# Attention values of a pair of heads on 64 columns of TensorE each, as plain float32 products

## The chip, the cores and the metric

The kernel runs on one core of one Trainium2 chip. The metric is the device time of one execution in microseconds (us). Engines are named as in the profile: PE (TensorE, matmuls), PEld (its weight loads), DVE (VectorE), ACT (ScalarE), POOL (GpSimd) and SP (which issues DMAs).

## The reference

The model is an encoder of two layers on 512 positions of width 1024. Each layer mixes by a Fourier branch of 512 channels and by windowed attention side by side, and then has a feed-forward part with a short convolution. The change is in the attention: 8 query heads of 64, 2 key and value heads, blocks of 128 queries against up to three neighbouring blocks of keys, and a learned sink in each softmax.

```python
def windowed_gqa(q, k, v, sink):
    ...
    scores = jnp.einsum("bnqkgd,bnjkd->bnkgqj", qb, kb).astype(jnp.float32) / math.sqrt(d)
    ...
    probs = jax.nn.softmax(jnp.concatenate([scores, sink_col], axis=-1), axis=-1)[..., :-1]
    out = jnp.einsum("bnkgqj,bnjkd->bnqkgd", probs.astype(v.dtype), vb)
    return out.reshape(b, s, N_HEADS * d)
```

The last einsum is the product of probabilities and values that the change rewrites. With four blocks of queries, the first and the last see two blocks of keys, the inner ones three: ten blocks of probabilities for each head.

## The kernel before

The activations lie transposed, channels on the 128 partitions and the 512 positions along the free dimension. Most products are made of float32 operands split into a high and a low float32r part: `mm3` (L114) then issues three matmuls, high by high (L120), high by low (L121) and low by high (L122). Where it gets a list of one operand, it issues one plain float32 matmul (L118). `split` (L98) makes the two parts, the high one by a copy on ACT (L90) and the low one by a subtraction on DVE (L93, or L96 with a scale); `put` (L107) does that for two parts, or one ACT copy for one part. In layer 0 the Fourier branch and the attention values are plain, in layer 1 they are split.

The heads are worked on in pairs (`attention`, L486): pair p has heads 2p and 2p+1 and one output bank `py` of PSUM, 128 rows by 512 positions, the first head's 64 channels above the second's. For each head and each query block, PE makes the scores (L506), DVE adds mask and scale and finds the maximum (L510), ACT takes exponentials and their sum (L513), DVE the reciprocal (L514), POOL multiplies (L515), PE transposes each 128x128 block of probabilities (L518), and `put` (L520) copies them from PSUM into `pT`. When a head's four blocks are through, four value products follow (L522 to L528), one for each block of keys, 256 or 384 queries wide. Their stationary operand is a slice of 128 columns of `vz`, a tile made by `zero_values` (L275) that holds the values of each key head between columns of zeros. Moved by 64, the slice puts the values into the upper or the lower 64 rows of `py` and adds zeros to the others, so both heads' products use all 128 columns and accumulate into one bank.

The order is that of the program, rearranged by a scheduler that simulates all engines when the program is built; each engine then works through its own list in order. Pair 3 is called between the two stages of the Fourier transform, pair 0 after it, pairs 1 and 2 after the Fourier output. The first half of the output projection (`proj`, L657) is tied to `steps`, the list of the transposes in the order of the program, so that its matmuls come between the blocks of the last pairs.

Of the kernel before, what the change touches and what calls it, by code (L numbers as in the profile page):

```python
# [8 lines left out]
F32 = mybir.dt.float32  # L9
F32R = mybir.dt.float32r  # L10
I32 = mybir.dt.int32
AF = mybir.ActivationFunctionType
ALU = mybir.AluOpType
# [3 lines left out]
P = 128  # L17
# [7 lines left out]
NB = S // P  # L25
# [12 lines left out]
def encoder_kernel(tc, t):  # L38
# [7 lines left out]
    nc = tc.nc  # L46
# [7 lines left out]
    cp = pool(name="const", bufs=1)  # L54
    wp = pool(name="weights", bufs=3)
    tp = pool(name="temps", bufs=2)
    sp = pool(name="small", bufs=2)
# [6 lines left out]
    def nm(s):  # L64
        uid[0] += 1
        return f"{s}_{uid[0]}"

    def f(x):
        return x.bitcast(F32)
# [6 lines left out]
    def psum(tag="mm"):  # L76
        return ps.tile([P, 512], F32, tag=tag, name=nm("ps"), bufs=BANKS[tag])

    def temp(n, tag, dt=F32):
        size, bufs = TEMPS[tag]  # L80
        return tp.tile([P, size], dt, tag=tag, name=nm(tag), bufs=bufs)[:, :n]
# [7 lines left out]
    def act(out, in_, func=AF.Copy, **kw):  # L89
        return nc.scalar.activation(out, in_, func, **kw)  # L90
# [16 lines left out]
    def put(dst, src, scale=None):  # L107

        if len(dst) == 2:
            split(dst[0], dst[1], src, scale=scale)  # L110
        else:
            act(dst[0], src, scale=1.0 if scale is None else scale)

    def mm3(out, a, b, start, stop, after=None, **kw):  # L114

        with tc.issue_after(after) if after is not None else nullcontext():
            if len(a) == 1:
                nc.tensor.matmul(out, a[0], b[0], start=start, stop=stop, **kw)  # L118
                return
            nc.tensor.matmul(out, a[0], b[0], start=start, stop=False, **kw)  # L120
            nc.tensor.matmul(out, a[1], b[0], start=False, stop=False, **kw)  # L121
            nc.tensor.matmul(out, a[0], b[1], start=False, stop=stop, **kw)  # L122
# [90 lines left out]
    def col_rstd(acc, inv, tag="tp"):  # L213

        pt = psum(tag)
        for b in range(NB):
            nc.tensor.matmul(pt[:, 2 * b:2 * b + 2], acc[:, b * P:(b + 1) * P], ones2, start=True, stop=True)  # L217
        return rsqrt(pt[:, 0:2 * NB:2], NB, inv, "n")
# [36 lines left out]
    mask = cut(pb, 3 * P)  # L255
# [10 lines left out]
    ident = cp.tile([P, P], F32, tag="ident", name="ident")  # L266
# [5 lines left out]
    nsink = cp.tile([P, L, NH], F32, tag="nsink", name="nsink")  # L272
    nc.vector.tensor_scalar(nsink, sink, -1.0, None, op0=ALU.mult)

    def zero_values(l):  # L275

        v = [cp.tile([P, NB, 320], F32R if l else F32, tag=f"vz{s}", name=nm("vz")) for s in range(1 + l)]
        for z in v:
            nc.gpsimd.memset(f(z) if l else z, 0.0)
        return v  # L280

    def load_tables(l):
        tab = []
        for i in range(2):
# [14 lines left out]
            nc.sync.dma_start(alt, t["alt"])  # L299
        return tab, alt  # L300

    vp = zero_values(0)


    def add_square(acc, src, first, tag="sq"):
# [47 lines left out]
    for l in range(L):  # L353

        r1 = col_rstd(acc, 1.0 / D)
        qraw = {}
        for grp in (1, 0):
            pq = [psum("mm" if b < 3 else "av") for b in range(NB)]
            for kk in range(KT // 2):
                if not l:  # L360
                    raw = first_w.pop(0) if first_w else wload(t["w_qkv"][l, grp, kk], 768)
                for k in (2 * kk, 2 * kk + 1):
                    if l:
                        w = fetch(f"qkv{grp}{k}", 384)
                    else:
                        w = wsplit(raw[:, (k % 2) * 384:(k % 2 + 1) * 384], hi_eng=nc.vector if grp == 1 else None)
                    for b in range(NB):
                        mm3(pq[b][:, :384], [xg[k][:, s, b * P:(b + 1) * P] for s in range(2)],
                            [w[s][:, :384] for s in range(2)], k == 0, k == KT - 1)
            if grp:  # L370
                rb1 = row_rstd(r1)
            z = temp(1536, "pT").rearrange("p (b c) -> p b c", b=NB)
            n = 256 if grp else 384
            for b in range(NB):
                act(z[:, b, :n], pq[b][:, :n], scale=r1[:, b:b + 1])
                if grp:
                    o = [v[:, b, 64:320].rearrange("p (g d) -> p g d", g=2)[:, :, :64] for v in vp]
                    put(o, pq[b][:, 256:384].rearrange("p (g d) -> p g d", g=2), r1[:, b:b + 1])
            for i in range(n // P):
                qraw[(3 if i == 0 else "k") if grp else i] = z[:, :, i * P:(i + 1) * P].rearrange("p b (h d) -> p b h d", h=2)  # L380

# [30 lines left out]
        qs_scale = {}  # L412
# [66 lines left out]


        accA = accum()
        off = [0, 2, 5, 8]
        steps = []
        ya = {}

        def attention(p, first_pair):  # L486
            g = p // 2
            py = psum("av")
            first = True
            if not l:  # L490
                both = temp(2560, "pT").rearrange("p (e b q) -> p e b q", e=2, q=P)
            for e in range(2):
                h = 2 * p + e
                nmax, den = [sp.tile([P, NB], F32, tag=z, name=nm(z), bufs=3) for z in ("nmax", "den")]
                if l:
                    pT = temp(2560, "pT", F32R).rearrange("p (s b q) -> p s b q", s=2, q=P)
                    pT = [pT[:, s] for s in range(2)]
                else:
                    pT = [both[:, e]]
                for i in range(NB):  # L500
                    j0, j1 = max(0, i - 1), min(NB - 1, i + 1)
                    n = (j1 - j0 + 1) * P
                    m0 = P if i == 0 else 0
                    sc = psum("sc")
                    for s in range(2):
                        nc.tensor.matmul(sc[:, :n], qT[p][:, e, i * P:(i + 1) * P], kT[g][:, s, j0 * P:(j1 + 1) * P],  # L506
                                         start=s == 0, stop=s == 1)
                    pr = temp(385, "tA")
                    nc.gpsimd.tensor_copy(pr[:, n:n + 1], nsink[:, l, h:h + 1])  # L509
                    nc.vector.tensor_tensor_reduce(  # L510
                        out=pr[:, :n], in0=sc[:, :n], in1=mask[:, m0:m0 + n], scale=qs_scale[p][:, i, e:e + 1],
                        scalar=nsink[:, l, h:h + 1], op0=ALU.add, op1=ALU.min, accum_out=nmax[:, i:i + 1])
                    act(pr[:, :n + 1], pr[:, :n + 1], AF.Exp, scale=-1.0, bias=nmax[:, i:i + 1], accum_out=den[:, i:i + 1])  # L513
                    nc.vector.reciprocal(den[:, i:i + 1], den[:, i:i + 1])  # L514
                    nc.gpsimd.tensor_scalar(pr[:, :n], pr[:, :n], den[:, i:i + 1], 1.0, op0=ALU.mult, op1=ALU.mult)  # L515
                    pp = psum("tp")
                    for j in range(n // P):
                        tr = nc.tensor.transpose(pp[:, j * P:(j + 1) * P], pr[:, j * P:(j + 1) * P], ident)  # L518
                    steps.append(tr.ins)
                    put([z[:, off[i]:off[i] + n // P, :].rearrange("p b q -> p (b q)") for z in pT], pp[:, :n])  # L520
                c0 = 128 * g + 64 * (1 - e)
                for j in range(NB):  # L522
                    i0, i1 = max(0, j - 1), min(NB - 1, j + 1)
                    st = off[i0] + j - max(0, i0 - 1)
                    rhs = [z[:, st:st + 2 * (i1 - i0) + 1:2, :] for z in pT]
                    lhs = [v[:, j, c0:c0 + P] for v in vp]
                    mm3(py[:, i0 * P:(i1 + 1) * P], lhs, rhs, first, e == 1 and j == NB - 1, skip_group_check=True)
                    first = False  # L528
            ya[p] = pair("act")
            split(ya[p][:, 0, :], ya[p][:, 1, :], py, scale=gA[:, l, p:p + 1])  # L530
            add_square(accA, py, first_pair)
# [6 lines left out]
        kT = turn_k(kss)  # L538
        qT = {3: turn_q(qs3, "m4")}
# [3 lines left out]
        for kk in range(KT // 2):  # L543
            if not l:
                wu = load_wu(l, kk)
            for k in (2 * kk, 2 * kk + 1):
# [3 lines left out]
                h = hs[k]  # L550
                st, sp_ = k == 0, k == KT - 1
# [25 lines left out]
        for stage in range(2):  # L577
            pe = [psum(), psum(), psum("sc")]
            po = psum()
            for m, (c0, c1) in enumerate(((0, 128), (128, 256), (256, 257))):  # L580
                o = pe[m][:c1 - c0, :258]
# [10 lines left out]
            for m in range(2):  # L592
                n = P - m
                o = po[:n, m * 256:(m + 1) * 256]
                for i in range(2):
# [3 lines left out]
                    st = m == 0 and i == 0  # L599
# [15 lines left out]
        for j in range(NF):  # L615
            pu = psum()
            pv = psum()
            c0, c1 = j * P, (j + 1) * P
# [60 lines left out]
        for mp in range(KT // 2):  # L679
            for i, w in enumerate(wo(1, mp)):  # L680
                m = 2 * mp + i
                o = proj((3, 0, 1, 2), ya, w, ("mm", "mm", "mm", "av", "sc", "sc", "mm", "mm")[m])
# [7 lines left out]
        acc = accum()  # L690
        if l == 0:
            tabs, alts = load_tables(1)
            vp = zero_values(1)
        ahead = presplit(l + 1) if l < L - 1 else iter(lambda: 0, 1)
        for f0, nf in HALVES:
            gu = []
            for fi in range(f0, f0 + nf):
                ys_ = []
                n = fi - f0
# [140 lines left out]
```

## Time and profile before

| | us |
|---|---|
| median of 3 runs (1074.64 to 1077.24) | 1075.63 |
| the profiled execution | 1076.12 |
| its span, first instruction to last | 1074.3 |
| DVE busy in the span | 737.2 |
| ACT busy in the span | 510.4 |

The execution shown by the profile is 0.49 us above the median, and 1.8 us of it lie outside the span. Lines are named L with their number in the kernel before. In a group of the profile, `out<-in` are the tiles' names without numbers, and `128*64 128x256` means 128 rows and 64 columns of the array in use and a product of 256 columns. PE records two instructions for one plain float32 product, one for a float32r matmul or a transpose. Since matmuls are pipelined, their recorded durations overlap; the distance from one start to the next tells how long PE was taken.

### The profile page before, as it was taken

How to read it: one execution, taken by the hardware profiler on the slowest of the kernel's cores; microseconds unless marked ns; L12 is line 12 of the kernel's file. 1: busy time of each engine (PE TensorE's matmuls, PEld its weight loads, DVE VectorE, ACT ScalarE, POOL GpSimd, SP SyncE). 2: the span in 40 equal slices, each digit the busy share in tenths (PEclk: the TensorE clock that was granted, in tenths of full speed). 3: DMA queues.
4: the chain of work that ended last, by engine and by line, in shares of the span. 5: the costliest groups of instructions: out<-in, count | busy, mean ns of one | idle time of the engine just before them, and what ended most of it. 6: DMA issues, size and time to landing. Idle time of an engine off the chain costs nothing.

```text
span 1074.3 us, 14345 instructions
## 1 busy us (share of the span) xinstructions
PE 1060.8 (99%) x5075; PEld 881.9 (82%) x5075; DVE 737.2 (69%) x1364; ACT 510.4 (48%) x940; POOL 118.4 (11%) x171
## 2 busy tenths in 40 slices
PE   8999999999999999999999999999999999999998
PEld 7866888888888888888899887888888888888887
DVE  7856767697767777776619788387887336777632
ACT  5338755454544445455414775155554224444421
POOL 1134410000000000000001442001211000101000
PEclk9999999999999999999999999999999999999999
DMA  7242162333259932338856322423332333233241
GB/s 276 83 138 84 36 196 79 99 98 98 86 174 372 367 99 97 99 104 297 299 182 212 112 70 79 138 79 99 98 99 81 101 106 100 85 102 94 81 147 47
DMA packets 58859, 142.13 MB, mean 132 GB/s; under 512 B 6554, under 2 KB 19108, under 8 KB 58788
## 3 DMA queue, kind: packets, MB, share of 16 engines
q1 hardware_dynamic: 58788, 141.22, 40.3%
q8 instruction: 40, 0.66, 0.3%
q14 instruction: 31, 0.25, 0.1%
HBM read 118.12 MB, written 23.07 MB: 131 GB/s over the span
## 4 chain that ended last, share of the span: by engine, by line
PE 92%; DVE 4%; ACT 1%; DMA 1%; issue 1%; SPq 0%; POOL 0%; DVEq 0%; ACTq 0%
PE ps L120 27%; PE ps L122 27%; PE ps L121 27%; PE ps L118 5%; PE ps L506 2%; PE ps L518 2%; DMA wraw<-in_w_qkv_dram 1%; DVE act L93 1%; PE ps L224 1%; DVE tF L96 1%; PE ps L217 1%; DVE tA L510 0%; PE ps L464 0%; DVE tF L93 0%; DVE slab L93 0%
## 5 line engine op out<-in xcount | busy, mean ns | idle before, releaser
L90 ACT ACTIVATE whi<-wraw 128x512 fp32r<-128x512 f32 (+1 forms) x296 | 181.9, 616 | 297.8 <-PE ps L122 281.4
L93 DVE TENSOR_TENSOR wlo<-wraw,whi 128x512 fp32r<-128x512 f32 (+1 forms) x304 | 221.9, 732 | 115.5 <-ACT whi L90 113.9
L120 PE MATMUL ps<-act,whi 128*128 128x512 f32 x768 | 298.9, 390 | 0.0
L121 PE MATMUL ps<-act,wlo 128*128 128x512 f32 x768 | 298.7, 389 | 0.0
L122 PE MATMUL ps<-act,whi 128*128 128x512 f32 x768 | 298.4, 389 | 0.0
L122 PEld LDWEIGHTS ps<-act,whi 128*128 128x128 f32 x768 | 144.2, 188 | 29.9
L121 PEld LDWEIGHTS ps<-act,wlo 128*128 128x128 f32 x768 | 144.2, 188 | 29.9
L120 PEld LDWEIGHTS ps<-act,whi 128*128 128x128 f32 x768 | 144.2, 188 | 29.8
L96 DVE SCALAR_TENSOR_TENSOR tF<-tF,pb,tF 128x511 f32<-128x511 f32 x176 | 133.2, 763 | 10.6 <-ACT tF L90 8.1
L93 DVE TENSOR_TENSOR tF<-ps,rb 128x512 f32<-128x512 f32 x104 | 71.1, 689 | 76.8 <-PE ps L122 65.2
L120 PE MATMUL ps<-slab,whi 128*128 128x512 f32 (+2 forms) x212 | 83.0, 391 | 1.4 <-ACT slab L90 1.4
L121 PE MATMUL ps<-slab,wlo 128*128 128x512 f32 (+2 forms) x212 | 81.0, 382 | 0.0
L122 PE MATMUL ps<-slab,whi 128*128 128x512 f32 (+2 forms) x212 | 81.0, 384 | 0.0
L90 ACT ACTIVATE tF<-tF,pb 128x512 f32<-128x512 f32 x88 | 71.5, 815 | 8.7 <-DVE tF L93 2.3
L93 POOL TENSOR_TENSOR tF<-tF,tF 128x512 f32<-128x512 f32 x22 | 29.6, 1347 | 257.5 <-DVE tF L96 244.8
L93 DVE TENSOR_TENSOR x<-x,ps 128x512 f32<-128x512 f32 (+1 forms) x49 | 32.9, 673 | 36.3 <-PE ps L122 36.2
L509 POOL COPY tA<-nsink 128x1 f32<-128x1 f32 x64 | 15.0, 243 | 356.8 <-DMA wraw<-in_w_down_dram 321.3
L120 PE MATMUL ps<-pT,whi 128*128 128x512 f32 (+1 forms) x132 | 50.9, 385 | 0.0
L121 PE MATMUL ps<-pT,wlo 128*128 128x512 f32 (+1 forms) x132 | 50.7, 384 | 0.0
L122 PE MATMUL ps<-pT,whi 128*128 128x512 f32 (+1 forms) x132 | 50.6, 383 | 0.0
L120 PEld LDWEIGHTS ps<-slab,whi 128*128 128x128 f32 x212 | 39.8, 188 | 9.4 <-ACT slab L90 1.6
L122 PEld LDWEIGHTS ps<-slab,whi 128*128 128x128 f32 x212 | 39.8, 188 | 8.6 <-DVE nmax L510 0.2
(171 smaller groups left out, 1589.7 us busy)
## 6 DMA issues: line engine op xcount, KB each, us to landing
wraw<-in_w_up_dram SPq DMA_DIRECT2D x88, 512.0 KB, 3.5
wraw<-in_w_down_dram SPq DMA_DIRECT2D x32, 512.0 KB, 3.5
kept<-tA SPq DMA_DIRECT2D x56, 256.0 KB, 5.5
whi<-kept SPq DMA_DIRECT2D x28, 256.0 KB, 2.9
wlo<-kept SPq DMA_DIRECT2D x28, 256.0 KB, 4.2
kept<-tA SPq DMA_DIRECT2D x32, 192.0 KB, 3.3
wraw<-in_w_down_dram SPq DMA_DIRECT2D x32, 192.0 KB, 3.3
wraw<-in_w_o_dram SPq DMA_DIRECT2D x8, 512.0 KB, 3.4
```

What stands on the lines that cost most here:

```text
L90: return nc.scalar.activation(out, in_, func, **kw)
L93: return (eng or nc.vector).tensor_tensor(out, a, b, op=op)
L96: return nc.vector.scalar_tensor_tensor(out=out, in0=a, scalar=s, in1=b, op0=op0, op1=op1)
L118: nc.tensor.matmul(out, a[0], b[0], start=start, stop=stop, **kw)
L120: nc.tensor.matmul(out, a[0], b[0], start=start, stop=False, **kw)
L121: nc.tensor.matmul(out, a[1], b[0], start=False, stop=False, **kw)
L122: nc.tensor.matmul(out, a[0], b[1], start=False, stop=stop, **kw)
L217: nc.tensor.matmul(pt[:, 2 * b:2 * b + 2], acc[:, b * P:(b + 1) * P], ones2, start=True, stop=True)
L224: nc.tensor.matmul(pt[:, b * P:(b + 1) * P], r[:, b:b + 1].to_broadcast([P, P]), ident, start=True, stop=True)
L506: nc.tensor.matmul(sc[:, :n], qT[p][:, e, i * P:(i + 1) * P], kT[g][:, s, j0 * P:(j1 + 1) * P], start=s == 0, stop=s == 1)
L509: nc.gpsimd.tensor_copy(pr[:, n:n + 1], nsink[:, l, h:h + 1])
L518: tr = nc.tensor.transpose(pp[:, j * P:(j + 1) * P], pr[:, j * P:(j + 1) * P], ident)
```

## The change

The values are kept once, unsplit and without zeros, as `vp` of 128 columns for each key block (64 for each key head), written by one ACT copy; `zero_values` and its three memsets go. In both layers the transposed probabilities are kept as plain float32, by one ACT copy; in layer 1 the subtraction on DVE goes. The value product of head e has 64 stationary columns and writes rows 64e to 64e+63 of `py`, so the two heads use different 64 columns of the array. The loops are turned round: two query blocks of both heads are brought to `pT`, then their value products follow, for three blocks of keys, the two heads by turns, 256 or 128 queries wide; then the other two blocks. The maxima and sums get a tile for each head.

```diff
-    def zero_values(l):
-        v = [cp.tile([P, NB, 320], F32R if l else F32, tag=f"vz{s}", name=nm("vz")) for s in range(1 + l)]
-        for z in v:
-            nc.gpsimd.memset(f(z) if l else z, 0.0)
-        return v
...
+        vp = cp.tile([P, NB, P], F32, tag="v", name=nm("v"))
...
-                    o = [v[:, b, 64:320].rearrange("p (g d) -> p g d", g=2)[:, :, :64] for v in vp]
-                    put(o, pq[b][:, 256:384].rearrange("p (g d) -> p g d", g=2), r1[:, b:b + 1])
+                    act(vp[:, b, :], pq[b][:, 256:384], scale=r1[:, b:b + 1])
...
-            for e in range(2):
-                h = 2 * p + e
-                nmax, den = [sp.tile([P, NB], F32, tag=z, name=nm(z), bufs=3) for z in ("nmax", "den")]
...
-                for i in range(NB):
+            stats = [[sp.tile([P, NB], F32, tag=f"{z}{e}", name=nm(z)) for z in ("nmax", "den")] for e in range(2)]
+            pT = temp(2560, "pT").rearrange("p (z e b q) -> p z e b q", z=2, e=2, q=P)
+            for half in range(2):
+                for i in (2 * half, 2 * half + 1):
...
+                    b0 = (0, 2, 0, 3)[i]
+                    for e in range(2):
...
-                    put([z[:, off[i]:off[i] + n // P, :].rearrange("p b q -> p (b q)") for z in pT], pp[:, :n])
-                c0 = 128 * g + 64 * (1 - e)
-                for j in range(NB):
-                    i0, i1 = max(0, j - 1), min(NB - 1, j + 1)
-                    st = off[i0] + j - max(0, i0 - 1)
-                    rhs = [z[:, st:st + 2 * (i1 - i0) + 1:2, :] for z in pT]
-                    lhs = [v[:, j, c0:c0 + P] for v in vp]
-                    mm3(py[:, i0 * P:(i1 + 1) * P], lhs, rhs, first, e == 1 and j == NB - 1, skip_group_check=True)
+                        act(pT[:, half, e, b0:b0 + n // P, :].rearrange("p b q -> p (b q)"), pp[:, :n])
+                for j in ((0, 1, 2), (1, 2, 3))[half]:
+                    i0, i1 = max(2 * half, j - 1), min(2 * half + 1, j + 1)
+                    b0 = (0, 2, 0, 3)[i0] + j - max(0, i0 - 1)
+                    for e in range(2):
+                        nc.tensor.matmul(py[64 * e:64 * e + 64, i0 * P:(i1 + 1) * P], vp[:, j, 64 * g:64 * g + 64],
+                                         pT[:, half, e, b0:b0 + 2 * (i1 - i0) + 1:2, :], start=(half, j) == (0, 0),
+                                         stop=(half, j) == (1, 3), skip_group_check=True)
```

Three places show what the change does to the engines' lists. The first is PE in layer 0, the first value products of pair 3. Before, L118 with `pT,vz` are value products, L506 scores, L518 transposes, and L118 with `tail` a piece of the Fourier output:

```order
L518 MATMUL ps_849<-ident,tA_843 128x128 x2
L118 MATMUL ps_795<-pT_796,vz_124 128x256
L506 MATMUL ps_949<-m_96_543,act_756 128x256 x2
L118 MATMUL ps_795<-pT_796,vz_124 128x384
L518 MATMUL ps_868<-ident,tA_862 128x128 x2
L506 MATMUL ps_962<-m_96_543,act_756 128x384 x2
L118 MATMUL ps_1074<-tail_943,wtr_1076 128x258
L506 MATMUL ps_976<-m_96_543,act_756 128x384 x2
L118 MATMUL ps_795<-pT_796,vz_124 128x384
L118 MATMUL ps_795<-pT_796,vz_124 128x256
```

In the list of the change the scores are L494, the transposes L506 and the value products L513, whose size begins with 64; rows of both heads read alike and are merged, so x3 is head 1, head 0, head 1:

```order
L506 MATMUL ps_849<-ident,tA_843 128x128 x3
L494 MATMUL ps_954<-m_96_542,act_755 128x256 x2
L513 MATMUL ps_794<-pT_799,v_180 64x256
L506 MATMUL ps_869<-ident,tA_863 128x128 x3
L494 MATMUL ps_967<-m_96_542,act_755 128x256 x2
L118 MATMUL ps_1081<-tail_946,wtr_1083 128x258
L494 MATMUL ps_980<-m_96_542,act_755 128x384 x2
L513 MATMUL ps_794<-pT_799,v_180 64x256 x3
L513 MATMUL ps_794<-pT_799,v_180 64x128 x2
L506 MATMUL ps_883<-ident,tA_877 128x128 x3
L506 MATMUL ps_897<-ident,tA_891 128x128 x2
L513 MATMUL ps_794<-pT_799,v_180 64x128
```

Before, the products of one head stand singly or in twos between other work of PE; now those of a half's two heads make a stretch of five, with single ones ahead of it and behind it, each between products on all 128 columns.

The second place is PE in layer 1, pair 1. Before, each value product is a triple of L120, L121 and L122:

```order
L120 MATMUL ps_6037<-pT_6040,vz_1868 128x256
L121 MATMUL ps_6037<-pT_6040,vz_1869 128x256
L122 MATMUL ps_6037<-pT_6040,vz_1868 128x256
L120 MATMUL ps_6037<-pT_6040,vz_1868 128x384
L121 MATMUL ps_6037<-pT_6040,vz_1869 128x384
L122 MATMUL ps_6037<-pT_6040,vz_1868 128x384
L120 MATMUL ps_6037<-pT_6040,vz_1868 128x384
L121 MATMUL ps_6037<-pT_6040,vz_1869 128x384
L518 MATMUL ps_6123<-ident,tA_6117 128x128 x2
L506 MATMUL ps_6409<-m_1240_5460,act_5807 128x256 x2
```

After, a stretch of pair 1 and two single products between transposes:

```order
L513 MATMUL ps_6327<-pT_6332,v_5108 64x256 x3
L513 MATMUL ps_6327<-pT_6332,v_5108 64x128 x2
L506 MATMUL ps_6416<-ident,tA_6410 128x128 x3
L506 MATMUL ps_6430<-ident,tA_6424 128x128 x2
L513 MATMUL ps_6327<-pT_6332,v_5108 64x128
L506 MATMUL ps_6443<-ident,tA_6437 128x128 x2
L513 MATMUL ps_6327<-pT_6332,v_5108 64x128
```

The triples have become pairs of products on 64 columns, as in layer 0. In the whole program the 96 value products of the change stand in 44 such unbroken stretches, 20 in layer 0 and 24 in layer 1. Of the products that are not the first of their stretch, 36 are 256 wide and 16 are 128. After 24 stretches PE goes on with transposes, after 20 with other work on the whole array.

The third place is DVE in layer 1, between the pairs 3 and 0. L510 makes the maxima, L514 reciprocals, and L93 with `pT` is the low half of the split of the probabilities:

```order
L93 TENSOR_TENSOR pT_5836<-ps_5846,pT_5836 128x256
L510 ISA tA_5957,nmax_5907<-ps_5954,pb,nsink,qknr_5440 128x256
L510 ISA nmax_5907 128x1
L514 RECIPROCAL den_5908<-den_5908 128x1
L93 TENSOR_TENSOR pT_5836<-ps_5860,pT_5836 128x384
L514 RECIPROCAL den_5908<-den_5908 128x1 x2
L96 SCALAR_TENSOR_TENSOR tail_6034<-ps_5986,tail_6034 1x258
L510 ISA tA_6044,nmax_6038<-ps_6041,pb,nsink,qknr_5771 128x256
L510 ISA nmax_6038 128x1
L93 TENSOR_TENSOR pT_5836<-ps_5875,pT_5836 128x384
L93 TENSOR_TENSOR pT_5836<-ps_5890,pT_5836 128x256
```

In the change L498 and L502 are maxima and reciprocals:

```order
L498 ISA tA_5951,nmax_5844<-ps_5948,pb,nsink,qknr_5448 128x256
L498 ISA nmax_5844 128x1
L502 RECIPROCAL den_5845<-den_5845 128x1
L502 RECIPROCAL den_5843<-den_5843 128x1
L502 RECIPROCAL den_5845<-den_5845 128x1
L96 SCALAR_TENSOR_TENSOR tail_6021<-ps_5973,tail_6021 1x258
L498 ISA tA_6033,nmax_6025<-ps_6030,pb,nsink,qknr_5779 128x256
L498 ISA nmax_6025 128x1
L502 RECIPROCAL den_6026<-den_6026 128x1
```

The subtractions into `pT` are gone, 32 of them in layer 1, and nothing has come in their place.

More of the change, by code (lines that the diff above doesn't have):

```diff
@@ L300, in load_tables @@
         return tab, alt
-    vp = zero_values(0)
     def add_square(acc, src, first, tag="sq"):
@@ L481, in encoder_kernel @@
         accA = accum()
-        off = [0, 2, 5, 8]
         steps = []
@@ L488, in attention @@
             py = psum("av")
-            first = True
-            if not l:
-                both = temp(2560, "pT").rearrange("p (e b q) -> p e b q", e=2, q=P)
-            for e in range(2):
-                h = 2 * p + e
-                nmax, den = [sp.tile([P, NB], F32, tag=z, name=nm(z), bufs=3) for z in ("nmax", "den")]
[L495 to L499, printed above, removed]
-                for i in range(NB):
+            stats = [[sp.tile([P, NB], F32, tag=f"{z}{e}", name=nm(z)) for z in ("nmax", "den")] for e in range(2)]
+            pT = temp(2560, "pT").rearrange("p (z e b q) -> p z e b q", z=2, e=2, q=P)
+            for half in range(2):
+                for i in (2 * half, 2 * half + 1):
                     j0, j1 = max(0, i - 1), min(NB - 1, i + 1)
@@ L503, in attention @@
                     m0 = P if i == 0 else 0
[L504 to L518, printed above, removed]
@@ L519, in attention @@
-                    steps.append(tr.ins)
-                    put([z[:, off[i]:off[i] + n // P, :].rearrange("p b q -> p (b q)") for z in pT], pp[:, :n])
-                c0 = 128 * g + 64 * (1 - e)
-                for j in range(NB):
-                    i0, i1 = max(0, j - 1), min(NB - 1, j + 1)
-                    st = off[i0] + j - max(0, i0 - 1)
-                    rhs = [z[:, st:st + 2 * (i1 - i0) + 1:2, :] for z in pT]
-                    lhs = [v[:, j, c0:c0 + P] for v in vp]
-                    mm3(py[:, i0 * P:(i1 + 1) * P], lhs, rhs, first, e == 1 and j == NB - 1, skip_group_check=True)
-                    first = False
+                    b0 = (0, 2, 0, 3)[i]
@@ new lines, in attention @@
+                    for e in range(2):
+                        h = 2 * p + e
+                        nmax, den = stats[e]
+                        sc = psum("sc")
+                        for s in range(2):
+                            nc.tensor.matmul(sc[:, :n], qT[p][:, e, i * P:(i + 1) * P], kT[g][:, s, j0 * P:(j1 + 1) * P],
+                                             start=s == 0, stop=s == 1)
+                        pr = temp(385, "tA")
+                        nc.gpsimd.tensor_copy(pr[:, n:n + 1], nsink[:, l, h:h + 1])
+                        nc.vector.tensor_tensor_reduce(
+                            out=pr[:, :n], in0=sc[:, :n], in1=mask[:, m0:m0 + n], scale=qs_scale[p][:, i, e:e + 1],
+                            scalar=nsink[:, l, h:h + 1], op0=ALU.add, op1=ALU.min, accum_out=nmax[:, i:i + 1])
+                        act(pr[:, :n + 1], pr[:, :n + 1], AF.Exp, scale=-1.0, bias=nmax[:, i:i + 1], accum_out=den[:, i:i + 1])
+                        nc.vector.reciprocal(den[:, i:i + 1], den[:, i:i + 1])
+                        nc.gpsimd.tensor_scalar(pr[:, :n], pr[:, :n], den[:, i:i + 1], 1.0, op0=ALU.mult, op1=ALU.mult)
+                        pp = psum("tp")
+                        for j in range(n // P):
+                            tr = nc.tensor.transpose(pp[:, j * P:(j + 1) * P], pr[:, j * P:(j + 1) * P], ident)
+                        steps.append(tr.ins)
+                        act(pT[:, half, e, b0:b0 + n // P, :].rearrange("p b q -> p (b q)"), pp[:, :n])
@@ L692, in encoder_kernel @@
             tabs, alts = load_tables(1)
-            vp = zero_values(1)
         ahead = presplit(l + 1) if l < L - 1 else iter(lambda: 0, 1)
```

## Prediction

> **What bounds the kernel now.** I read the page first: busy shares, then the chain of work that ended last.
>
> ```profile
> PE 1060.8 (99%) x5075; PEld 881.9 (82%) x5075; DVE 737.2 (69%) x1364; ACT 510.4 (48%) x940; POOL 118.4 (11%) x171
> ...
> PE 92%; DVE 4%; ACT 1%; DMA 1%; issue 1%; SPq 0%; POOL 0%; DVEq 0%; ACTq 0%
> ```
>
> PE is busy 99% of the span and makes 92% of the chain, so time on PE is time of the kernel, unless it falls into a wait. The change lies in the attention of both layers, so the next view is the table of stretches, for attention of layer 0 (88 to 130 us), of layer 1 (600 to 676 us), and for the part of the latter where PE waits most.
>
> ```profile
> core 0: us, PE busy (x) PEld busy (x) DVE busy (x) ACT busy (x) POOL busy (x), PEclk, DMA share, GB/s
> 88.00:130.00 42.00, 40.62 (x220) 30.48 (x219) 32.24 (x106) 37.62 (x104) 21.68 (x50) 1.00 0.20 64
> 600.00:676.00 76.00, 73.20 (x464) 62.34 (x464) 58.68 (x182) 52.22 (x141) 24.42 (x60) 1.00 0.20 61
> 630.00:652.00 22.00, 19.51 (x124) 16.44 (x125) 20.09 (x61) 17.68 (x47) 9.59 (x23) 1.00 0.10 33
> ```
>
> PE idles 1.4 us in the first, 2.8 us in the second, and 2.5 us of those 2.8 lie between 630 and 652 us, where DVE is busy 20.09 of 22 us. So PE's own work is the first thing to count, DVE's in layer 1 the second.
>
> **The value products themselves.** The view of one tile gives their number, before:
>
> ```profile
> L118 PE MATMUL ps<-pT,vz x64: 377/432/569, 94.2 to 153.7; 128*128 128x256 f32 x32, 128*128 128x384 f32 x32
> ...
> L120 PE MATMUL ps<-pT,vz x32: 277/334/445, 617.5 to 678.5; 128*128 128x256 f32 x16, 128*128 128x384 f32 x16
> ```
>
> Layer 0 (L118) has 64 records for 32 products: a plain float32 product is two passes. Layer 1 (L120, and as many of L121 and L122) has 32 products of three float32r matmuls each. Durations overlap, so I price them by the distance between starts, in the timeline:
>
> ```profile
> 97.29 1.24 PE L118 MATMUL ps<-pT,vz 128*128 128x384 f32 x4
> 98.36 0.71 PE L518 MATMUL ps<-ident,tA 128*128 128x128 f32 x5
> ```
>
> for layer 0, and for layer 1
>
> ```profile
> 649.89 0.28 PE L121 MATMUL ps<-pT,vz 128*128 128x256 f32 x1
> 650.01 0.28 PE L122 MATMUL ps<-pT,vz 128*128 128x256 f32 x1
> 650.12 0.34 PE L120 MATMUL ps<-pT,vz 128*128 128x384 f32 x1
> 650.30 0.33 PE L121 MATMUL ps<-pT,vz 128*128 128x384 f32 x1
> ```
>
> The first row merges two passes of 384 columns with two of 256: 1280 columns in 1.07 us, 0.836 ns a column of a plain pass (0.214 us for 256, 0.107 for 128). A float32r matmul takes 0.12 us for 256 and 0.18 for 384. Layer 0 before: 32 x 256 + 32 x 384 = 20480 columns, 17.1 us. Layer 1 before: 48 x 0.12 + 48 x 0.175 = 14.2 us. Together **31.3 us**.
>
> After, both layers have plain products alone: 64 of 256 columns and 32 of 128, two passes each, 40960 columns, 34.2 us if they follow each other. That is the upper end: **+2.9 us**, all of it from layer 1, where two plain passes cost four thirds of three float32r ones. If the two heads' products, which lie on different 64 columns of the array, ran wholly side by side, they would take 17.1 us: **-14.2 us**, the lower end. No row here has two products on different columns, so neither end is shown. Between them I go by how passes are issued. The order of after is head 0, head 1 by turns, and each product's two passes need the same columns one after the other; so the second pass of one head can run beside the first pass of the other, and not more. The nearest rows, an excursion to a product with one column of the array in layer 0, show when weights are loaded; the columns are start, length, engine, line, operation and, ahead of the size, rows*columns of the array in use:
>
> ```profile
> 54.01 0.60 PE L118 MATMUL ps<-whi,slab 128*128 128x258 f32 x2
> 54.54 0.60 PE L118 MATMUL ps<-whi,slab 128*1 128x258 f32 x2
> 55.07 0.70 PE L118 MATMUL ps<-whi,slab 128*128 128x256 f32 x2
> ```
>
> and of PE's weight loads in the same stretch
>
> ```profile
> 54.54 0.09 PEld L118 LDWEIGHTS ps<-whi,slab 128*1 128x1 f32 x2 [0.34 <-issue]
> 55.06 1.16 PEld L118 LDWEIGHTS ps<-whi,slab 128*128 128x128 f32 x6 [0.44 <-issue]
> ```
>
> The two one-column loads span 0.09 us from 54.54, so the second was issued as the first pass began: one load ahead. And an uncovered load of 128 columns shows as 0.70 against 0.60 for two passes: 0.10 us, so some 0.053 for 64 (an estimate, half of it). A following product then costs one pass plus 0.053 us instead of two passes: 0.161 us saved with 256 columns, 0.054 with 128. In the order of after the 96 products stand in 44 unbroken stretches; of the 52 that are not first in theirs, 36 have 256 columns and 16 have 128: 36 x 0.161 + 16 x 0.054 = 6.7 us saved, 27.5 us left, **-3.8 us** against before. I take this.
>
> The Trainium skill (TensorE: Matmul & The Clock Gate, Part 3: Packing small matmuls) says that products on different column groups run concurrently and gives 2.38 times for three of them. No run here shows it; scaled to two (1.59 times, an estimate from that page) the products would take 21.5 us and the forecast below would be 1077.9 us.
>
> **The changes of shape.** The rows above show a price that the diff doesn't: going from 128*128 to 128*1 and back. From 54.01 to 55.07 are four passes of 258 columns, 0.863 us by the rate above, but 1.06 us passed: 0.20 us; and the load uncovered on return adds the 0.10 us. So **0.29 us an excursion** in plain float32. In layer 1 two more kinds stand:
>
> ```profile
> 629.05 0.52 PE L506 MATMUL ps<-m,act 128*128 128x384 f32 x2
> 629.50 0.38 PE L121 MATMUL ps<-tail,wt 1*128 1x258 f32 x1
> 629.72 0.28 PE L122 MATMUL ps<-tail,wt 1*128 1x258 f32 x1
> 629.92 0.51 PE L506 MATMUL ps<-m,act 128*128 128x256 f32 x2
> 630.27 0.34 PE L122 MATMUL ps<-pT,vz 128*128 128x384 f32 x1
> ```
>
> ```profile
> 587.95 0.64 PE L120 MATMUL ps<-whi,slab 128*128 128x258 f32 x4
> 588.43 0.28 PE L121 MATMUL ps<-whi,slab 128*128 128x258 f32 x1
> ```
>
> ```profile
> L120 PE MATMUL ps<-whi,slab 128*1 128x258 f32 x8 | 2.2, 281 | 0.0
> ```
>
> One row of the array (1*128, float32r): 1.22 us for 2 x 0.18 + 4 x 0.12 = 0.83, so 0.39 us. One column in float32r: the four from 587.95, of which one is such a 128*1 product, take 0.48 us, 0.12 each: nothing. The new products are plain float32 and use 64 columns, so the nearest is the 0.29; with 64 instead of one column to load on the way in it is 0.32 (0.29 + 0.053, less about 0.02 because 24 of the 44 returns are to transposes). 44 x 0.32 = **+14.1 us**, between 0 (the float32r row) and 44 x 0.39 = 17.2.
>
> The Trainium skill (TensorEngine Tiling (Array Packing), Key Properties) says that a change of tiling mode drains TensorE, whatever the type, and this speaks against the change. The 0.29 and 0.39 agree; the free float32r column doesn't. By the rule the term stays at 14.1 us, by the free row it is nothing, which is the second rival below.
>
> **DVE in layer 1.** The second half of each split of the transposed probabilities goes; ACT keeps its copy.
>
> ```profile
> L93 DVE TENSOR_TENSOR pT<-ps,pT 128x256 fp32r<-128x256 f32 (+1 forms) x32 | 15.1, 479 | 3.4 <-ACT pT L90 3.4
> ```
>
> The waits of 630 to 652 us, and the chain of work there:
>
> ```profile
> PE ps L120 <- ACT slab L90: 1.4, 1, 1.4
> ...
> PE ps L518 <- DVE pT L93: 1.0, 2, 0.7
> ```
>
> ```profile
> 645.16 2.07 DVE tF L96 x3
> 647.23 0.33 DVE pT L93
> ```
>
> 32 x 0.479 = 15.1 us of DVE work goes. PE can gain only what it waits: 0 to 2.8 us, the idle time of the stage. Both named waits end in DVE's chain (the three L96, then the splits), so I take **-2.0 us**. What is late next is the score's own reduction on DVE (L510), which stays.
>
> **At nothing.** The three memsets run on POOL (11% busy); the values' low half is four short DVE instructions; the values' copy stays on ACT. A half's products wait for both heads' copies, and behind them on PE stand the next transposes and scores; before, a head's products waited for as many blocks, and copies of two pairs fit into the buffers of pT as well as the maxima and sums. SP issues the same DMAs, a few places apart. If this cover went, a wait of one block's chain would come per pair, already inside PE's waits of 1.4 and 1.0 us.
>
> **Sum.** The profiled execution took 1076.12 us (span 1074.3). 1076.1 - 3.8 + 14.1 - 2.0 = 1084.4; it stands 0.5 above the median 1075.63, so 1083.9, **1084 us**, 0.8% slower.
>
> **Rivals.**
> - *No sharing*: the two heads' products follow each other, so the change doesn't do what it says. For it: no row shows two at once, and all PE starts are in order. Against it: nothing. 1076.1 + 2.9 + 14.1 - 2.0 - 0.5 = 1090.6 us.
> - *Shape changes are free*, the other side. For it: the float32r 128*1 row. Against it: the plain 128*1 rows, same type as the new ones. It decides the sign: with sharing 1076.1 - 3.8 - 2.0 - 0.5 = 1069.8 us, faster once an excursion costs under (3.8 + 2.0) / 44 = 0.13 us; without sharing 1076.5.
> - *Full sharing*: 17.1 us for the products. It needs weights of one head loaded beside the other's pass, more than the one load ahead that the rows show. 1076.1 - 14.2 + 14.1 - 2.0 - 0.5 = 1073.5 us.
>
> **Chances.** Forecast 0.45, no sharing 0.27, free shape changes 0.14 (0.09 with sharing), full sharing 0.14. A measurement of this kernel can tell about 0.2%, 2.2 us, from no change. Faster by more: 0.09, and half of full sharing: 0.16. Same: 0.05, the other half, and 0.03 of the forecast's edge: 0.15. Slower: 0.69. The range 1072 to 1092 us leaves out free changes with sharing below and the edge of no sharing with 0.39 us an excursion above; the forecast's own range is 1079 to 1088.
>
> **What would show it.** Products on 64 columns whose second head starts about 0.05 us after the first's second pass mean sharing; 0.21 us after, none; with it, full sharing. A first pass in a stretch that starts about 0.1 us late, and again the first one behind it, mean shape changes are paid. In layer 1 the wait at 645 us should be gone. A wrong count of stretches would not matter, for the order is fixed; a wrong price of an excursion would: 0.1 us is 4.4 us.

## The result, and the profile after

The changed kernel took **1078.75 us** (median of 5 runs, 1078.0 to 1080.3) against 1075.63 us (5 runs) before: ratio 1.0032, 95% interval 1.0019 to 1.0045. A second measurement beside later kernels, for which the same 3.1 us had been expected, gave 1077.45 us (11 runs) against 1076.19 (20 runs): 1.3 us, ratio 1.0017 (1.0008 to 1.0025). It is slower, by 0.2 to 0.3% and not by the forecast 0.8%. The time lies inside the range, the direction was right, the size was not.

The page of the changed kernel, where scores are now L494, transposes L506 and value products L513:

```profile
PE 1067.2 (99%) x5107; PEld 871.8 (81%) x5107; DVE 723.7 (67%) x1328; ACT 508.8 (47%) x940; POOL 114.1 (11%) x168
...
PE 96%; DVE 1%; DMA 1%; ACT 1%; issue 0%; SPq 0%; POOL 0%; DVEq 0%; ACTq 0%; POOLq 0%
```

PE's share of the chain rose from 92 to 96% and DVE's fell from 4 to 1%. The stretches of the prediction, after (columns as there):

```profile
88.00:130.00 42.00, 40.57 (x248) 27.69 (x247) 31.43 (x106) 37.32 (x106) 22.75 (x53) 1.00 0.21 64
600.00:676.00 76.00, 75.55 (x460) 55.81 (x459) 45.33 (x149) 50.99 (x141) 26.63 (x60) 1.00 0.18 58
630.00:652.00 22.00, 21.64 (x135) 15.30 (x133) 15.54 (x60) 18.51 (x54) 11.00 (x28) 1.00 0.15 49
...
0.00:84.28 84.28, 78.83 (x380) 65.38 (x380) 59.76 (x151) 33.76 (x69) 13.93 (x15) 0.96 0.48 158
84.28:163.61 79.33, 77.32 (x424) 54.63 (x425) 56.46 (x160) 57.56 (x152) 26.82 (x59) 1.00 0.33 107
163.61:554.16 390.55, 390.55 (x1738) 322.87 (x1736) 278.90 (x447) 188.25 (x298) 3.59 (x8) 1.00 0.51 169
554.16:691.11 136.95, 136.36 (x838) 111.13 (x838) 81.57 (x230) 70.69 (x180) 38.06 (x62) 1.00 0.40 127
691.11:1078.50 387.39, 384.12 (x1732) 317.84 (x1730) 247.06 (x340) 158.57 (x243) 31.71 (x24) 1.00 0.31 95
```

DVE lost 13.3 us in layer 1 (45.33 against 58.68), and PE's idle time there fell from 2.8 to 0.45 us. The last five rows cut the run at points that every kernel has: layer 0's first score product, the column sums of squares behind its output projection (L217), the same sums that open layer 1, and those behind layer 1's projection. The second and fourth are the two attention stages. The same five cuts before:

```profile
0.00:82.75 82.75, 77.57 (x381) 64.53 (x381) 59.52 (x151) 33.75 (x69) 18.64 (x17) 0.98 0.48 161
82.75:161.71 78.96, 76.79 (x392) 59.53 (x393) 56.41 (x160) 58.35 (x152) 27.27 (x60) 1.00 0.34 107
161.71:552.26 390.55, 390.55 (x1738) 322.85 (x1736) 278.52 (x447) 188.18 (x298) 3.44 (x8) 1.00 0.50 169
552.26:686.90 134.64, 131.73 (x837) 117.09 (x837) 95.72 (x266) 71.50 (x180) 37.36 (x62) 1.00 0.41 129
686.90:1074.30 387.40, 384.12 (x1732) 317.85 (x1730) 247.04 (x340) 158.57 (x243) 31.67 (x24) 1.00 0.31 95
```

Outside the attention nothing moved (390.55 and 390.55, 387.40 and 387.39). The attention grew by 0.37 us in layer 0 and 2.31 in layer 1, **2.7 us** in all; the remaining 1.5 us of the profiled execution lie in the opening, where the granted clock was 0.96 instead of 0.98. In the second profiled execution of the changed kernel the opening took 81.78 us and the stages 79.33 and 136.94 us again. So the stages repeat and the opening scatters (by 2.5 us between these two), and the sums below are made by stages.

What the stages hold is seen in the timeline of PE after, around the first lone product and the first long stretch of pair 3:

```profile
95.46 0.55 PE L506 MATMUL ps<-ident,tA 128*128 128x128 f32 x3
95.77 0.48 PE L494 MATMUL ps<-m,act 128*128 128x256 f32 x2
96.17 0.65 PE L513 MATMUL ps<-pT,v 128*64 128x256 f32 x2
96.75 0.55 PE L506 MATMUL ps<-ident,tA 128*128 128x128 f32 x3
97.05 0.48 PE L494 MATMUL ps<-m,act 128*128 128x256 f32 x2
...
98.64 1.30 PE L513 MATMUL ps<-pT,v 128*64 128x256 f32 x10
99.87 0.33 PE L506 MATMUL ps<-ident,tA 128*128 128x128 f32 x1
```

The lone product holds PE 0.58 us up to the next start, where its two passes are worth 0.43. But the stretch of ten passes (six of 256 columns, four of 128, 1.71 us at 0.836 ns a column) is over in 1.23. Its starts in the trace, in us, one row for each pass:

```
98.640  256 columns        98.647  256 columns (other head)
98.907  256                98.914  256
99.123  256                99.130  128
99.339  256                99.239  128
99.555  128
99.664  128                99.867  next: transpose
```

The two heads' passes start **7 ns apart**, not one pass apart. Each head's passes follow each other as if the other head weren't there; the second row is later by one uncovered weight load, 0.053 us.

All 44 stretches, from the distances of starts (which give about 0.216 us for a pass of 256 columns and 0.108 for 128): 26 are lone products and take 9.55 us where their passes one after the other would take 8.21. The other 18 take 17.36 us instead of 26.31. Together 26.9 us instead of 34.5. Entering a stretch costs 0.10 us more than the product ahead of it needs, leaving it 0.098, and the next product's uncovered load 0.08 (12.3 us for 44); with the 0.053 of the first load, which is inside the 26.9, an excursion costs **0.33 us**, 14.6 us in all.

### The profile page after: what moved, and what is told of

It reads as the page before. It is cut to its first block, busy times and chain, and to the rows that moved or that the text cites. A ratio compares the mean times of both kernels' runs of the same rounds, so it can differ in the third digit from the quotient of the medians.

```text
span 1078.5 us, 14376 instructions
## 1 busy us (share of the span) xinstructions
PE 1067.2 (99%) x5107; PEld 871.8 (81%) x5107; DVE 723.7 (67%) x1328; ACT 508.8 (47%) x940; POOL 114.1 (11%) x168
## 4 chain that ended last, share of the span: by engine, by line
PE 96%; DVE 1%; DMA 1%; ACT 1%; issue 0%; SPq 0%; POOL 0%; DVEq 0%; ACTq 0%; POOLq 0%
PE ps L120 28%; PE ps L121 28%; PE ps L122 28%; PE ps L118 4%; PE ps L513 3%; PE ps L506 2%; PE ps L494 2%; PE ps L224 1%; DMA x<-in_xT_dram 1%; PE ps L217 1%; PE ps L456 0%; PE ps L467 0%; PE ps L576 0%; ACT tA L90 0%; DMA wraw<-in_w_qkv_dram 0%
## 5 line engine op out<-in xcount | busy, mean ns | idle before, releaser
L93 DVE TENSOR_TENSOR wlo<-wraw,whi 128x512 fp32r<-128x512 f32 (+1 forms) x304 | 221.8, 732 | 117.5 <-ACT whi L90 116.1
L120 PE MATMUL ps<-act,whi 128*128 128x512 f32 x768 | 298.9, 390 | 0.0
L121 PE MATMUL ps<-act,wlo 128*128 128x512 f32 x768 | 298.7, 389 | 0.0
L122 PE MATMUL ps<-act,whi 128*128 128x512 f32 x768 | 298.4, 389 | 0.0
L122 PEld LDWEIGHTS ps<-act,whi 128*128 128x128 f32 x768 | 144.2, 188 | 30.0
L121 PEld LDWEIGHTS ps<-act,wlo 128*128 128x128 f32 x768 | 144.2, 188 | 30.0
L120 PEld LDWEIGHTS ps<-act,whi 128*128 128x128 f32 x768 | 144.2, 188 | 29.6
L93 DVE TENSOR_TENSOR tF<-ps,rb 128x512 f32<-128x512 f32 x104 | 71.1, 689 | 76.8 <-PE ps L122 65.2
L120 PE MATMUL ps<-slab,whi 128*128 128x512 f32 (+2 forms) x212 | 82.3, 388 | 0.0
L121 PE MATMUL ps<-slab,wlo 128*128 128x512 f32 (+2 forms) x212 | 81.2, 383 | 0.0
L122 PE MATMUL ps<-slab,whi 128*128 128x512 f32 (+2 forms) x212 | 80.7, 384 | 0.0
L93 DVE TENSOR_TENSOR x<-x,ps 128x512 f32<-128x512 f32 (+1 forms) x49 | 33.0, 676 | 50.2 <-PE ps L122 50.0
L93 POOL TENSOR_TENSOR tF<-tF,tF 128x512 f32<-128x512 f32 x22 | 29.7, 1349 | 257.4 <-DVE tF L96 244.8
L120 PE MATMUL ps<-pT,whi 128*128 128x512 f32 (+1 forms) x132 | 50.9, 385 | 0.0
L121 PE MATMUL ps<-pT,wlo 128*128 128x512 f32 (+1 forms) x132 | 50.7, 384 | 0.0
L122 PE MATMUL ps<-pT,whi 128*128 128x512 f32 (+1 forms) x132 | 50.6, 383 | 0.0
L498 DVE CUSTOM_DVE_ANT_0 tA<-ps,pb,nsink 128x256 f32<-128x256 f32 (+1 forms) x64 | 38.2, 604 | 18.2 <-PE ps L494 13.9
L121 PEld LDWEIGHTS ps<-slab,wlo 128*128 128x128 f32 x212 | 39.8, 188 | 9.7 <-issue 1.5
```

Of the source, the lines that this page charges most:

```text
L93: return (eng or nc.vector).tensor_tensor(out, a, b, op=op)
L498: nc.vector.tensor_tensor_reduce(out=pr[:, :n], in0=sc[:, :n], in1=mask[:, m0:m0 + n], scale=qs_scale[p][:, i, e:e + 1], scalar=nsink[:, l ...
```

## The theories after the result

*Main theory (M)*: the halves run fully side by side within a stretch (24.6 us for the products, first loads apart); an excursion costs 0.33 us; freeing DVE in layer 1 is worth nearly 5 us. *Rival (F)*: the forecast's own terms hold (6.7 us saved by sharing, 14.1 paid for shapes, 2.0 from DVE) and something not seen gives the rest back. *Loops only* (L): what costs time is the new order of loops, and DVE's work doesn't matter. The expectations use these names; W in experiment 4 stands for waits that come back.

In the experiments 1, 2, 3 and 5 the edit also moves some of PE's other work: the scheduler built another order of PE's list for each, in the stages that the edit touches. A difference of stages holds that too.

## Experiments

**1. The new loops, with all 128 columns.** The change's loops and plain float32 stay; the values lie between columns of zeros again, so there is neither sharing nor a change of shape.

```diff
-        vp = cp.tile([P, NB, P], F32, tag="v", name=nm("v"))
+        vp = cp.tile([P, NB, 320], F32, tag="v", name=nm("v"))
+        nc.gpsimd.memset(vp, 0.0)
...
-                        nc.tensor.matmul(py[64 * e:64 * e + 64, i0 * P:(i1 + 1) * P], vp[:, j, 64 * g:64 * g + 64],
+                        c0 = 128 * g + 64 * (1 - e)
+                        nc.tensor.matmul(py[:, i0 * P:(i1 + 1) * P], vp[:, j, c0:c0 + P],
...
```

> The changed kernel's loops and plain float32 in both layers, but each value product again on all 128 columns, with the values between zeros: no change of shape, no two products side by side. Theory M (from the trace of the changed kernel: its 44 stretches hold PE 26.9 us and 12.3 us more go into and out of them, 39.2 us in all): the products take 34.2 us, 5.0 less, 1073.8 us. Rival F (the forecast's terms, 27.5 + 14.1 = 41.6 us, and an unknown gain of about 5 us elsewhere): 34.2 in place of 41.6, 1071.4 us. If neither shape nor sharing matters and the time comes from the loops: 1078.8 us.

Measured 1075.21 us (11 runs) against 1074.86 (21 runs): ratio 0.9998 (0.9989 to 1.0007). The stages are 79.03 and 133.59 us, so putting the products on 64 columns costs 0.30 + 3.36 = 3.7 us. M's terms give 12.3 - (34.5 - 26.9) = 4.7, F's 7.4; loops only would have left this kernel at the change's time, and it falls. M's 1073.8 us was missed by 1.4, and of its 4.7 us one is not explained; the list of this kernel has 42 stretches instead of 44, and its order differs. The excursion can be compared row by row, in this kernel's timeline of PE at the same lone product (scores L496, transposes L508, values L516):

```profile
92.80 0.48 PE L496 MATMUL ps<-m,act 128*128 128x256 f32 x2
93.12 0.59 PE L516 MATMUL ps<-pT,v 128*128 128x256 f32 x2
93.55 0.49 PE L508 MATMUL ps<-ident,tA 128*128 128x128 f32 x3
93.80 0.48 PE L496 MATMUL ps<-m,act 128*128 128x256 f32 x2
```

From start to start: scores 0.32 us (0.40 with 64 columns), product 0.43 (0.58), transposes 0.25 (0.30). That is 0.08 + 0.15 + 0.05 = 0.28 us for one excursion, between the same neighbours.

**2. The kernel before, with plain float32 in layer 1.** Old loops, 128 columns, no low half: the DVE term alone, less the 2.9 us that plain passes cost.

```diff
-        v = [cp.tile([P, NB, 320], F32R if l else F32, tag=f"vz{s}", name=nm("vz")) for s in range(1 + l)]
+        v = [cp.tile([P, NB, 320], F32, tag="vz0", name=nm("vz"))]
...
-                if l:
-                    pT = temp(2560, "pT", F32R).rearrange("p (s b q) -> p s b q", s=2, q=P)
-                    pT = [pT[:, s] for s in range(2)]
-                else:
-                    pT = [both[:, e]]
+                pT = [both[:, e]]
```

> The kernel before, old loops, all 128 columns, only layer 1's values and probabilities plain float32 as in layer 0. It isolates the 32 subtractions on DVE. Products in layer 1 cost 17.1 for 14.2 us, +2.9 us. Theory M (DVE's relief is worth 4.7 us): 1075.6 + 2.9 - 4.7 = 1073.8 us, and the same as the run with the new loops on 128 columns. Rival F (relief 2.0 us): 1076.5 us. Rival L (the turned loops are what shortens layer 1, not DVE's work): 1078.5 us.

Measured 1073.0 us (11 runs), ratio 0.9983 (0.9975 to 0.9992): 1.9 us faster. With 2.9 us more of streaming on PE, the relief is **4.8 us**; by the stage of layer 1 (133.02 us instead of 134.64) it is 4.5. M had also expected the time of experiment 1; that kernel is 2.2 us slower by the medians, and 0.6 by the two stages (212.62 against 211.98). The 600 to 676 us of this kernel:

```profile
600.00:676.00 76.00, 76.00 (x442) 62.00 (x443) 47.15 (x151) 51.55 (x141) 23.97 (x60) 1.00 0.21 65
```

PE's recorded idle time went from 2.8 us to none, yet the relief was 4.8: the record of idle time was no upper bound. The rows show why. A pass of 256 columns is recorded as 0.38 to 0.43 us, the next starts 0.214 us after it, and so some 0.2 us of each wait lies under a recorded end. The longest wait of the kernel before:

```profile
644.64 0.50 PE L506 MATMUL ps<-m,act 128*128 128x256 f32 x2
646.55 0.50 PE L120 MATMUL ps<-slab,whi 128*128 128x512 f32 x1 [1.41 <-ACT slab L90]
```

From start to start it is 1.91 us for two float32r matmuls that are worth 0.24, so PE is 1.67 us late where the record has 1.41. Summed over layer 1, PE's starts are 5.2 us late before and 0.8 us here, if each is held against the shortest distance that the same three instructions in a row show anywhere in these traces (differences over 0.04 us, counted outside the value products): 4.4 us, in agreement with the relief.

**3. The change, with the subtraction on DVE put back.** 32 subtractions like those of before, into a tile that nothing reads.

```diff
+        dump = cp.tile([P, 384], F32R, tag="dump", name=nm("dump"))
...
+                        if l:
+                            tt(dump[:, :n], pp[:, :n], pT[:, half, e, b0:b0 + n // P, :].rearrange("p b q -> p (b q)"), ALU.subtract)
```

> The changed kernel with the 32 subtractions of layer 1 put back on DVE, into a tile that nobody reads: PE's list and the output stay. Theory M: the relief is given back, +4.7 us, 1083.4 us, less what the new loops hide. Rival F: +2.0, 1080.8 us. Rival L (DVE's work doesn't matter): 1078.8 us.

Measured 1081.92 us (5 runs), ratio 1.0066 (1.0053 to 1.0078), 3.9 us above the change's first measurement and 5.8 above its second (each against the kernel before); by the stages 2.9, all of it in layer 1 (139.85 against 136.95). So DVE's work still counts under the new loops, by the stages by more than F's 2.0 and by less than 4.8; that the longer way of PE hides the rest is likely, but not shown. The waits on PE return, in the view of waits from 590 to 700 us:

```profile
PE ps L122 <- DVE slab L93: 1.0, 1, 1.0
PE ps L120 <- ACT slab L90: 0.9, 1, 0.9
PE ps L516 <- ACT pT L90: 0.4, 2, 0.3
```

where the changed kernel has one wait of 0.2 us.

**4. One stretch for a pair.** All value products of a pair come after its last transpose, heads by turns, 256 or 384 columns wide: 8 excursions instead of 44, each with two full halves.

```diff
-                for j in ((0, 1, 2), (1, 2, 3))[half]:
-                    i0, i1 = max(2 * half, j - 1), min(2 * half + 1, j + 1)
...
+            prev = steps[-1]
+            for n, (e, j) in enumerate([(e, j) for j in (3, 2, 1, 0) for e in (1, 0)]):
+                i0, i1 = max(0, j - 1), min(NB - 1, j + 1)
+                b0 = (0, 2, 5, 8)[i0] + j - max(0, i0 - 1)
+                with tc.issue_after(prev):
+                    prev = nc.tensor.matmul(py[64 * e:64 * e + 64, i0 * P:(i1 + 1) * P], vp[:, j, 64 * g:64 * g + 64],
+                                            pT[:, e, b0:b0 + 2 * (i1 - i0) + 1:2, :], start=j == 3, stop=j == 0,
...
```

> The changed kernel with all eight value products of a pair (256 or 384 wide, heads by turns) held back until the pair's last transpose and issued as one stretch: 8 stretches in place of 44. Theory M: the two heads' products run wholly side by side, 17.1 us, and 8 x 0.33 us go into and out of the stretches, 19.8 in place of 39.2: 1059.4 us. Rival F (one load ahead, so only a pass of each product is covered): 22.2 + 2.6 = 24.8 us, 1064.4 us. Rival W (the products of a pair now wait for its last copy, PE idles, and the next pair's buffers come free later): the gain is given back in part or whole, 1068 us or more.

Measured **1064.95 us** (4 runs), ratio 0.9904 (0.9890 to 0.9917): 9.9 us faster than before, and the best kernel here. Its timeline of PE (values L514):

```profile
101.76 2.37 PE L514 MATMUL ps<-pT,v 128*64 128x256 f32 x16
104.07 0.44 PE L506 MATMUL ps<-ident,tA 128*128 128x128 f32 x2
```

Sixteen passes, 5120 columns or 4.28 us one after the other, are over in 2.31 us including the way out: half. The stages are 74.85 and 128.37 us. M's 1059.4 was missed by 5.5 us. F's 1064.4 is nearest to the time, but by luck: its 24.8 us are 3.1 for each stretch with the way in and out, where the trace has 2.5 (2.31, and 0.18 around it). What M left out are waits that the changed kernel didn't have. In the view of waits, layer 1 (590 to 700 us):

```profile
PE ps L514 <- ACT pT L90: 0.7, 1, 0.7
PE ps L494 <- DVE nmax L498: 0.7, 3, 0.3
```

and in layer 0 two rows of the same kind with 0.4 and 0.8 us. Two of the eight stretches stood at the head of PE's list until the last copy had landed: this order trades excursions for a few waits. The recorded ones are some 3 us; by the distances of starts, counted as in experiment 2, PE is 9.0 us late in the two stages and 4.9 in those of the changed kernel, so some 4 of the 5.5 us are waits, 2.8 of them in layer 0. The other 1.4 us are open.

**5. The same, with the stretch broken.** After each second product stands a float32r product of 2 columns on all 128x128 of the array that adds zeros, 24 in all: 24 more excursions and next to nothing to stream.

```diff
+                if n in (2, 4, 6):
+                    with tc.issue_after(prev):
+                        prev = nc.tensor.matmul(py[:, 384:386], zz, zz[:, :2], start=False, stop=False,
...
```

> The kernel with one stretch of eight value products a pair, with a product of zeros (two columns wide, all 128 columns of the array, float32r) put after each second product, so that each stretch becomes four: 24 more excursions, each pair of the two heads' products still together, nothing else changed; the zeros add nothing to the output. Theory M (an excursion costs 0.29 to 0.34 us, as in the trace of the changed kernel): 24 x 0.33 and about 0.07 for each zero product, +9.6 us on the 1064.9 of the unsplit run, 1074.5 us. If an excursion costs nothing and the gain of the single stretch came from elsewhere: +1.7, 1066.6 us.

Measured 1071.13 us (6 runs) against 1076.19 (20 runs): ratio 0.9958 (0.9943 to 0.9973), so 5.1 us faster than before instead of 9.9: **4.8 us** for the 24, with an uncertainty of some 2 us from the two intervals. PE's timeline:

```profile
105.64 0.65 PE L520 MATMUL ps<-pT,v 128*64 128x256 f32 x4
106.23 0.27 PE L517 MATMUL ps<-zz 128*128 128x2 f32 x1
106.43 0.87 PE L520 MATMUL ps<-pT,v 128*64 128x384 f32 x4
107.23 0.27 PE L517 MATMUL ps<-zz 128*128 128x2 f32 x1
107.43 0.87 PE L520 MATMUL ps<-pT,v 128*64 128x384 f32 x4
```

Four passes of 256 columns in two halves are worth 0.43 us; the next stretch starts 0.79 us after them: 0.36 us for going out and in, 8.6 us for 24, and all 24 in the trace are alike (0.35 to 0.36 us, the zero product included, for which the expectation had put down 0.07 more). The price on PE is thus shown without a change of the value products, of the loops or of DVE's work; the product between the stretches is float32r. That only 4.8 us arrived fits the waits that it fills: in layer 1 the two waits of 1.4 us above are one of 0.3 here, and the stage grew by 2.84 us for 12 x 0.36 = 4.3. The "free" theory (1.7 us) falls, and M's 9.6 counted too little cover. (Layer 0 of this profiled execution ran at a mean granted clock of 0.77 from 90 to 112 us, so its stage isn't used; from 104 us on, where the rows above stand, it was 1.00.)

**6. One stretch, listed head by head.** The products of experiment 4, but four of one head and then four of the other: only the order of the list changes.

```diff
-            for n, (e, j) in enumerate([(e, j) for j in (3, 2, 1, 0) for e in (1, 0)]):
+            for n, (e, j) in enumerate([(e, j) for e in (1, 0) for j in (3, 2, 1, 0)]):
```

> The kernel with one stretch a pair, but the four products of the second head first, then the four of the first: the same products, no alternation. If the two halves of the array take their products independently however they are ordered: 1064.9 us as with alternation, 2.21 us a stretch. If a product can only start beside its next neighbours in the list, as the forecast's one load ahead had it, hardly anything is shared: up to 4.30 us a stretch, 8 x 2.1 = 16.7 more, 1081.6 us; something between would give the depth to which the list is searched.

Measured 1073.48 us (8 runs), ratio 0.9974 (0.9964 to 0.9984), 7.2 us behind experiment 4 (each against the kernel before). The same stretch in its timeline:

```profile
99.81 3.50 PE L514 MATMUL ps<-pT,v 128*64 128x256 f32 x16
103.25 0.44 PE L506 MATMUL ps<-ident,tA 128*128 128x128 f32 x2
```

3.44 us against 2.31; 8 x 1.13 = 9.0 us, and the stages' sum is 9.1 longer. The trace's starts say how: the first head's passes start at 99.814, 100.080, 100.296, 100.619 and 100.941, the second head's first at 100.947, 6 ns after the first head's fifth. So a pass four entries further down the list starts before the three ahead of it (101.264, 101.586, 101.802), and one further away does not. Its operands were there: both heads' last copies into pT had ended by 99.70 us. Both ends of the expectation fall, 1064.9 us for halves that are independent of the order and 1081.6 for hardly any sharing. The Trainium skill (TensorE: Matmul & The Clock Gate, Part 3: Packing small matmuls) says that matmuls start in program order; between two halves of the array this trace shows otherwise. So PE works through its list in order on each half, but not across the two.

## Why the prediction was off

| term, us | forecast | trace and runs |
|---|---|---|
| value products, first loads apart | -3.8 | -6.7 (31.3 to 24.6) |
| 44 excursions | +14.1 | +14.6 |
| DVE in layer 1 | -2.0 | -4.8 |
| sum | +8.3 | +3.1 |
| both attention stages, measured | | +2.7 |

That 3.1 comes so near to 2.7 is in part luck: by the stages of experiment 1 the columns cost 3.7 us instead of 4.7, and the new loops keep 3.9 us of DVE's relief instead of 4.8 (212.62 - 213.60 = 2.9 - 3.9), two differences that cancel.

- **Direction: right, and for the stated reason.** The price of the changes of shape outweighs what sharing saves and what DVE's relief adds, but two gains, both put too small, took away 5.7 of the 8.3 us forecast. The one-column excursion of the plain rows (0.29 us, with the load 0.32) was the right neighbour, and the float32r row that costs nothing was not: 0.33 from the stretches, 0.28 in one pair of rows, 0.36 between two stretches. The rule of the Trainium skill weighed there (TensorEngine Tiling (Array Packing), Key Properties), which gives no figure and names no type, agrees with all three in that there is a price.
- **The value products: the step that failed is "the second pass of one head can run beside the first pass of the other, and not more".** It was read from one row with a load issued as the first pass began, all of it in one shape and so with every pass on the same columns. The trace shows 7 ns between the heads. The rival of full sharing had the mechanism, but its 17.1 us supposed that every product has a partner. 26 of 44 stretches are lone products, and in a stretch of five the third product of one head ends alone: so 24.6, where the forecast had 27.5. Of the prediction's three signs for the second head's start (0.05 us after the first's second pass, 0.21 us after it, or with it), the trace shows the last wherever there is a second head. A slip stands beside it without effect on the sum: by the prediction's own rates two plain passes cost 1.2 times three float32r ones (0.428 against 0.36 us for 256 columns), not four thirds.
- **DVE: the bound failed, "PE can gain only what it waits: 0 to 2.8 us".** Experiment 2 gives 4.8. The recorded idle time leaves out what lies under the modelled ends of matmuls; the distances between starts give some 4.4.
- **At nothing: held, in the main.** The wait at 645 us is gone, as forecast, the profile records one wait of 0.2 us in layer 1, and POOL, the four values' copies and SP show nowhere. By the distances of starts PE is still about 1.1 us late between 646 and 650 us, which neither experiment 1 nor 2 shows to that extent.
- **What stays open:** one microsecond of the columns' price in experiment 1, 1.4 us of experiment 4, and how much of the relief the change keeps (4.8 in the old loops, by the stages 2.9 to 3.9 in the new ones).

## What to carry to other kernels

Two plain float32 products on different halves of the array's columns cost the time of one, if they stand by turns in the list and in long stretches. Each stretch costs a third of a microsecond, so a lone product loses, and two of 256 columns, one on each half, gain hardly anything (0.43 us saved for 0.33). Count the stretches in the built order before the products: with DVE relieved in both, the same columns made the kernel 1 to 3 us slower in 44 stretches and 10 us faster in 8. And take what a busy engine could gain from the distances of starts, not from its recorded idle time. Add them up over a few instructions: in experiment 2 a float32r matmul behind a plain pass of 256 columns is recorded 0.03 us after it and the next one 0.31 us later, and only together are these the 0.33 us that the two are worth.

## What was not expected of the hardware

- Plain float32 products of two passes on two halves of the array run wholly side by side, 5 to 7 ns apart: 2.31 us for 4.28 us of passes.
- How far ahead PE looks for work on free columns is short: listed head by head, the second half began only with the first half's fifth pass, 1.13 us late.
- A lone product on 64 columns is slower than the same product with zeros on the other 64: 0.58 against 0.43 us from start to start.
